# Grouped-query attention on one core: the last job's exponentials, the closing checks, the last store and the general path's loads moved between engines

## The chip, the core and the metric

The kernel runs on one core of a Trainium2 chip. A core has five engines with queues of their own: TensorE (PE in the profile; its weight loads are PEld), VectorE (DVE), ScalarE (ACT), GpSimd (POOL) and SyncE (SP), which only issues DMAs here. Each engine takes its instructions in program order and waits for others by semaphores. Matrix products go to PSUM, which VectorE and ScalarE read; all else lies in SBUF.

The metric is the device time of one execution in microseconds (us), the median of several. Lower is better.

## What is computed

Attention with 32 query heads that share 8 heads of keys and values, four query heads to one; batch 8, sequence 512, head size 64, all in float32:

```python
K_expanded = np.repeat(K, heads_per_group, axis=2)
V_expanded = np.repeat(V, heads_per_group, axis=2)
scores = np.einsum('bhqd,bhkd->bhqk', Q, K_expanded) * scale     # scale = 1/sqrt(64)
weights = np.exp(scores - np.max(scores, axis=-1, keepdims=True))
weights = weights / (np.sum(weights, axis=-1, keepdims=True) + 1e-10)
output = np.einsum('bhqk,bhkd->bhqd', weights, V_expanded)       # heads moved to axis 1
```

The inputs are normally distributed random numbers.

## The kernel before, in words

There are two paths. `fast_path` computes the output without subtracting the maximum: it takes the exponential of the scaled scores as they are, in fp16. While it does so it checks that every row sum lies between `SUM_LO` and `SUM_HI`, and that the largest absolute value in V is at most `V_HI`. The checks end in one number, the tile `flag` ([1, 1]). After the fast path `values_load` (L54) loads the flag into a register of every engine, and `tc.If` (L55) jumps over `general_path`, which would compute everything again with the maximum subtracted. With these inputs the jump is always taken.

**Jobs.** The fast path is a loop over 64 jobs. Job j is one head of keys and values in one batch (u = j // 2 counts pairs of such heads, `b` is the batch, eight jobs to a batch), with its four query heads taken as two pairs, i = 0 and 1. One job needs 16 score blocks of 128 keys x 512 queries per half (`m`): for each pair i and key chunk kc of four, two matmuls (L221, two heads at a time in the upper and lower 64 rows) write a tile of 128 x 1024 in PSUM.

**Exponentials.** Most tiles go to ScalarE, one ACTIVATE for each tile of 1024 columns (`act_tile`, L239), which writes `pt` in fp16. The PSUM pool `sps` has two such tiles. A few blocks of pair 1 go to VectorE and GpSimd instead (`taken(j)`: 2 blocks of 512 columns, or 3 in the even jobs from 8 on). These form the exponential from the bits of an fp16 number: VectorE makes `u` from the scores (`exp_d`, L250) and masks `f` (`exp_d2`, L271); GpSimd makes `g` and `w` (`correction`, L263 and L267); VectorE adds u and w and so writes those blocks of `pt` (`exp_d4`, L284), one job later. In job 63, the last, `by_pool` is false, and VectorE does g and w too, in the same job. With three blocks taken, ScalarE has seven tiles in a job, one of them half as wide; with two, seven full ones.

**Products with V.** `pv(j, i, lo, hi)` (L315) multiplies the blocks of `pt` with V, 32 small matmuls for each pair, 16 at a time in between the scores of the next job; a column of ones in V gives the row sums. `norm(j, i)` takes the reciprocal of the sums on VectorE (L358), multiplies (L362) into `osb`, and stores from SyncE's queue (`store`, L402): one store for each u, but in the last u one for each pair of heads. The order of keys in the products is written out in `blocks`.

**Checks.** `check_v` (L195) reduces a quarter of V's batch to its largest absolute value on VectorE. `check_sums` compares 16 norms' reciprocals at a time with both bounds (`in_bounds`, L326). After the norm that leaves `NLAST` = 3 more, the rest is checked, and `vmax` (L378), `okmin` (L380) and `okall` (L381) gather all that came before. `last_check`, called by the last norm between its reciprocal and its multiplication, compares the last three norms (24 columns) in two VectorE instructions, counts over the 128 partitions by a matmul with ones (L396), and the very last instruction reduces the counts to the flag by their minimum (L537).

**Order of work.** `tc.manual_schedule()` keeps each engine's instructions in the order in which the program emits them, so the loop body is the order, written out by hand. Within a job it is: scores for tile 0, blocks for VectorE, tile 1, a check of V, then the products of the job before between the tiles. Loads of Q, K and V are issued from GpSimd's queue, three jobs or more ahead; the transposed keys and the stores are on SyncE's.

**The close.** What follows the flag has the lines of the program's own frame: L54 is the load of the flag, L55 the jump and the semaphores that stand for the skipped branch, L650 the end of the program, at which all engines meet.

Of the kernel before, what the change touches and what calls it, by code (L numbers as in the profile page):

```python
# [3 lines left out]

# [7 lines left out]
FP32 = mybir.dt.float32  # L12
# [6 lines left out]
EXP = mybir.ActivationFunctionType.Exp  # L19
AX = mybir.AxisListType  # L20
# [13 lines left out]
V_HI = 1.0e15  # L34

# [4 lines left out]
@with_exitstack  # L40
def kernel(
    ctx: ExitStack,
    tc: tile.TileContext,
    Q: bass.AP,
    K: bass.AP,
    V: bass.AP,
    out: bass.AP,
):
    nc = tc.nc
    flag_pool = ctx.enter_context(tc.tile_pool(name="flag", bufs=1))  # L50
    flag = flag_pool.tile([1, 1], I32, name="flag")
    with ExitStack() as fast, tc.manual_schedule():
        fast_path(fast, tc, Q, K, V, out, flag)
    good = nc.values_load(flag, min_val=0, max_val=128)  # L54
    with tc.If(good < 128):  # L55
        general_path(tc, Q, K, V, out)


def fast_path(ctx, tc, Q, K, V, out, flag):
# [28 lines left out]
    ident = const_pool.tile([128, 128], BF16, name="ident")  # L88
# [45 lines left out]
    def d_tile():  # L134
        return d_pool.tile([128, 2, S], FP32, name="d_ps")
# [69 lines left out]
    def taken(j):  # L205
        return 3 if WIDE(j) else 2
# [8 lines left out]
    jobs, osb, invs, ends = {}, {}, {}, []  # L215
# [40 lines left out]
    def by_pool(j):  # L256
        return j < NJOB - 1

    def correction(engine, f, g, w):
        as_bits = engine is nc.gpsimd
        engine.tensor_scalar(  # L263
            out=g, in0=f, scalar1=-EXP_F1, scalar2=EXP_K * 2.0 ** (24 * as_bits),
            op0=ALU.add, op1=ALU.mult,
        )
        engine.tensor_tensor(out=w, in0=g, in1=f.bitcast(FP16) if as_bits else f, op=ALU.mult)  # L267

    def exp_d2(j):
        st = jobs[j]  # L270
        nc.vector.tensor_single_scalar(  # L271
            out=st["f"], in_=st["u"], scalar=1023, op=ALU.bitwise_and
        )
        if by_pool(j):
            exp_d3(j, nc.gpsimd)

    def exp_d3(j, engine):
        st = jobs[j]
        correction(engine, st["f"], st["g"], st["w"])
# [13 lines left out]
    def blocks(j, i):  # L293
        if j == NJOB - 1:
            kcs = (0, 1, 2, 3) if i == 0 else (2, 0, 1, 3)
# [27 lines left out]
    def in_bounds(outs, inv, first):  # L323
        ops = ((1.0 / SUM_HI, ALU.is_ge), (1.0 / SUM_LO, ALU.is_le))
        for out_, in1, (bound, op) in zip(outs, (first, outs[0]), ops):
            nc.vector.scalar_tensor_tensor(  # L326
                out=out_, in0=inv, scalar=bound, in1=in1, op0=op, op1=ALU.mult
            )
# [11 lines left out]
    NLAST = 3  # L340
    inv_last = const_pool.tile([128, NLAST, 2, SC], FP32, name="inv_last")

    def norm(j, i):
# [15 lines left out]
        if left == 1:  # L359
            last_check()  # L360
        h = g * HPG + 2 * i
        nc.vector.tensor_tensor(  # L362
            out=osb[u][:, :, h:h + 2, :].rearrange("p qc m d -> p m qc d"),
            in0=sums[:, :, :, 0:D],
            in1=inv[:, :, :, None].to_broadcast((128, 2, SC, D)),
            op=ALU.mult,
        )
# [18 lines left out]
    def last_check():  # L386
        cols = NLAST * 2 * SC
        part = const_pool.tile([128, cols], FP32, name="part")
        right = const_pool.tile([128, cols], BF16, name="right")
        in_bounds(  # L390
            (part, right),
            inv_last.rearrange("p s m qc -> p (s m qc)"),
            okall[:, :].to_broadcast((128, cols)),
        )
        count = pv_pool.tile([128, 2, S], FP32, name="pv")
        nc.tensor.matmul(count[0:1, 0, 0:cols], ones, right, start=True, stop=True)  # L396
        ends.append(count[0:1, 0, 0:cols])

    def store(u, lo, hi):
        b, gp = divmod(u, GP)  # L400
        h0 = gp * 2 * HPG
        nc.sync.dma_start(  # L402
            out=out[b, :, h0 + lo:h0 + hi, :].rearrange("(sc p) h d -> p sc h d", p=128),
            in_=osb[u][:, :, lo:hi, :],
        )

# [39 lines left out]
    for j in range(NJOB):  # L446
        end = j == NJOB - 1
# [42 lines left out]
        if not end:  # L490
            bank = d_tile() if j else pv_tile()
            beside = act_tile(j, 4, bank) if taken(j) > 2 else None

            ahead = (j + 1,) if j < 6 else (7, 8) if j == 6 else (j + 2,)
            for n, to in enumerate(ahead):
                if to < NJOB:
                    reads.append(trans_q(to, bank[:, n, :], other=beside))
            if j == 0:
                reads.append(first_keys(1, bank[:, 1, :]))
            elif j == 1:  # L500
                reads.append(first_k(1, 1, bank[:, 1, :]))
            elif j > 1 and b == 0 and gp + 1 < GP:
                reads.append(first_k(gp + 1, g, bank[:, 1, :]))
        else:
            pv(j, 0, 0, 16)
        copies = [] if by_pool(j) else [read() for read in reads]
        if late and by_pool(last):
            exp_d4(last)
        check_sums()
        exp_d2(j)  # L510
        if not by_pool(j):
            exp_d3(j, nc.vector)
            exp_d4(j)
        else:
            copies = [read() for read in reads]
# [5 lines left out]
        if not end and taken(j + 1) > 2:  # L521
            exp_d(j + 1, 2, taken(j + 1), bank[:, 1:2, :], copies[0])()
# [9 lines left out]
        if end:  # L532
            pv(j, 0, 16, 32)
            norm(j, 0)
            pv(j, 1, 0, 32)
            norm(j, 1)
    nc.vector.tensor_reduce(out=flag, in_=ends[0], op=ALU.min, axis=AX.X)  # L537


def general_path(tc, Q, K, V, out):  # L540
# [8 lines left out]
    with ExitStack() as ctx:  # L549
        one = ctx.enter_context(tc.tile_pool(name="g_one", bufs=1))  # L550
        sb = ctx.enter_context(tc.tile_pool(name="g_sb", bufs=2))
        ps = ctx.enter_context(tc.tile_pool(name="g_ps", bufs=2, space=PS))
        ident = one.tile([128, 128], BF16, name="g_ident")
        make_identity(nc, ident)
        with tc.For_i(0, B, 1) as b:
            with tc.For_i(0, KV, 1) as g:
                k_nat = sb.tile([128, SC, D], BF16, name="g_k")
                v_nat = sb.tile([128, SC, D], BF16, name="g_v")
                for tile_, src in ((k_nat, K), (v_nat, V)):
                    nc.gpsimd.dma_start(  # L560
                        out=tile_,
                        in_=src[bass.ds(b, 1), :, bass.ds(g, 1), :].rearrange(
                            "o (sc p) g d -> p (o sc) (g d)", p=128
                        ),
                    )
                kt_ps = ps.tile([64, SC, 128], BF16, name="g_t")
# [4 lines left out]
                with tc.For_i(0, HPG, 1) as i:  # L571
                    q_nat = sb.tile([128, SC, D], BF16, name="g_q")
                    nc.gpsimd.dma_start(
                        out=q_nat,
# [3 lines left out]
                    )  # L578
                    o_sb = sb.tile([128, SC, D], FP32, name="g_o")
# [75 lines left out]
```

## Time and profile before

| | before |
|---|---|
| median of 3 runs | 417.14 us (417.1 to 418.14) |
| the profiled execution | 417.43 us |
| its span in the profile | 415.8 us |
| granted TensorE clock over the span | 0.996 |
| ScalarE busy | 400.6 us (96%) |
| PE busy (modelled) | 378.1 us (91%) |
| VectorE busy | 342.6 us (82%) |
| GpSimd busy | 301.5 us (73%) |

How to read the rows below. In a group of the page stand the line, the engine, the operation, the tiles written and read with their shapes, and the count; then the busy time in us and the mean of one in ns; then the engine's idle time ahead of them and what ended most of it. In the timeline stand the start in us, the length in us (of several instructions merged, from the first start to the last end), then the group. An engine's name with a q, as POOLq, is its queue: loads of registers, jumps, semaphores and the issue of DMAs, which do not count as busy. Records of one engine overlap, since each holds the instruction's whole way through the engine.

### The profile page before, as it was taken

Reading aid. Unit: us, or ns where it says so; the run is one execution under the profiler, and the core shown is the slowest. Engines: PE = TensorE matmul, PEld = TensorE weight load, DVE = VectorE, ACT = ScalarE, POOL = GpSimd, SP = SyncE. Lnnn points to the kernel's source line nnn. Section 1 sums busy time; section 2 is a strip of 40 time slices with the busy share of each in tenths; the row PEclk is TensorE's granted clock in tenths of the full one; section 3 lists DMA queues with packets and bytes.
Section 4 is the critical chain, followed back from the end, with each engine's and each line's share of the span. In section 5 each row is a group of like instructions: output and inputs, shape, how many; then the busy total and the mean of one; then the engine's idle time right before and its main releaser. Section 6 shows DMA issues by size and latency. Waiting matters only on the chain.

```text
span 415.8 us, 13054 instructions
## 1 busy us (share of the span) xinstructions
PE 378.1 (91%) x5681; PEld 233.7 (56%) x5681; DVE 342.6 (82%) x609; ACT 400.6 (96%) x449; POOL 301.5 (73%) x213
## 2 busy tenths in 40 slices
PE   5899999999999999999999999999999999999983
PEld 2555655555655555655655655555655555655652
DVE  3677888888888888988888888888889888898875
ACT  3999999999999999999999999999999999999992
POOL 9677665887678886797776897587876887667550
PEclk9999999999999999999999999999999999999998
DMA  9999976799849997399974999669995899732223
GB/s 136 162 165 188 191 154 153 107 214 187 171 139 205 127 222 160 114 217 130 240 181 94 208 180 215 159 85 219 188 173 151 173 160 213 162 110 102 102 102 107
DMA packets 91966, 67.20 MB, mean 162 GB/s; under 512 B 52097, under 2 KB 75137, under 8 KB 91905
## 3 DMA queue, kind: packets, MB, share of 16 engines
q0 software_dynamic: 55488, 24.91, 51.8%
q1 hardware_dynamic: 35888, 41.16, 36.1%
q8 instruction: 45, 0.74, 0.7%
q10 hardware_dynamic: 528, 0.26, 0.2%
q14 instruction: 17, 0.13, 0.1%
HBM read 50.33 MB, written 33.55 MB: 202 GB/s over the span
## 4 chain that ended last, share of the span: by engine, by line
ACT 84%; PE 10%; DVE 3%; issue 1%; DMA 1%; ACTq 0%; DVEq 0%
ACT pt L239 84%; PE s_ps L221 6%; PE pv L315 3%; DMA kf<-in_K_dram 1%; DVE o_sb L362 1%; DVE pt L284 1%; PE pv L185 1%; PE d_ps L185 1%; DVE qt L189 0%; DVE ok L326 0%; ACTq L239 0%; DVE w L267 0%; DVE f L271 0%; PE d_ps L146 0%; DVE twice L153 0%
## 5 line engine op out<-in xcount | busy, mean ns | idle before, releaser
L239 ACT ACTIVATE pt<-s_ps 128x1024 f16<-128x1024 f32 x420 | 397.4, 1289 | 6.1 <-PE s_ps L221 6.1
L315 PEld LDWEIGHTS <-pt 128*128 128x128 f16 x4096 | 142.1, 98 | 75.7 <-issue 56.1
L315 PE MATMUL pv<-v,pt 128*128 128x65 bf16 x4032 | 178.2, 195 | 1.0 <-DVE o_sb L362 0.5
L267 POOL TENSOR_TENSOR w<-g,f 128x1024 bf16<-128x1024 bf16 (+1 forms) x63 | 161.0, 2555 | 5.2
L221 PE MATMUL s_ps<-qt,kt 64*128 64x512 bf16 x728 | 142.6, 383 | 22.3 <-ACT pt L239 16.3
L263 POOL TENSOR_SCALAR g<-f 128x1024 bf16<-128x1024 int16 (+1 forms) x63 | 77.4, 1229 | 96.6 <-DVE f L271 96.6
L250 DVE TENSOR_SCALAR u<-d_ps 128x1024 int16<-128x1024 f32 (+1 forms) x92 | 96.8, 1052 | 1.1 <-PE d_ps L221 1.1
L362 DVE TENSOR_TENSOR o_sb<-pv,inv 128x512 f32<-128x512 f32 x125 | 86.4, 691 | 4.3
L221 PEld LDWEIGHTS <-kt 64*128 64x128 bf16 x896 | 51.8, 93 | 62.3 <-issue 34.9
L358 DVE RECIPROCAL inv<-pv 128x8 f32<-128x8 f32 x125 | 25.9, 207 | 54.6 <-PE pv L315 54.5
L284 DVE TENSOR_TENSOR pt<-u,w 128x1536 uint16<-128x1536 int16 (+1 forms) x64 | 51.1, 798 | 0.1
L221 PE MATMUL d_ps<-qt,kt 64*128 64x512 bf16 x168 | 43.0, 375 | 0.0
L189 DVE COPY qt<-d_ps 128x1024 bf16<-128x1024 bf16 x62 | 42.3, 684 | 0.0
L185 PEld LDWEIGHTS <-q_nat 128*128 128x128 bf16 x512 | 29.3, 99 | 21.1 <-issue 20.0
L185 PE MATMUL d_ps<-ident,q_nat 128*128 128x128 bf16 x496 | 38.3, 220 | 0.0
L271 DVE TENSOR_SCALAR f<-u 128x1536 int16<-128x1536 int16 (+1 forms) x64 | 30.6, 478 | 0.0
L114 POOL DMA_DIRECT2D v<-in_V_dram x32 | 29.0, 909 | 0.1
L129 POOL DMA_DIRECT2D q_nat<-in_Q_dram x33 | 27.0, 818 | 0.2 <-issue 0.2
L221 PE MATMUL s_ps<-qt,kt_first 64*128 64x512 bf16 x112 | 23.1, 407 | 4.2 <-ACT pt L239 3.0
L239 ACT ACTIVATE pt<-d_ps 128x512 f16<-128x512 f32 x28 | 25.2, 899 | 0.0
L195 DVE TENSOR_REDUCE okv<-v 128x1 f32<-128x512 bf16 x32 | 21.6, 676 | 0.0
L221 PEld LDWEIGHTS <-kt_first 64*128 64x128 bf16 x128 | 7.9, 95 | 11.9 <-issue 8.3
(52 smaller groups left out, 44.5 us busy)
## 6 DMA issues: line engine op xcount, KB each, us to landing
out_dram<-o_sb SPq DMA_DIRECT2D x31, 1024.0 KB, 6.8
q_nat<-in_Q_dram POOLq DMA_DIRECT2D x31, 512.0 KB, 6.2
k_nat<-in_K_dram POOLq DMA_DIRECT2D x7, 512.0 KB, 8.3
v<-in_V_dram POOLq DMA_DIRECT2D x28, 128.0 KB, 7.5
kt<-kt SPq DMA_DIRECT2D x14, 256.0 KB, 4.6
out_dram<-o_sb SPq DMA_DIRECT2D x4, 256.0 KB, 2.4
kt<-k_nat SPq DMA_TRANSPOSE x28, 5.8
v<-in_V_dram POOLq DMA_DIRECT2D x4, 96.0 KB, 8.4
```

Of the source, the lines that this page charges most:

```text
L114: nc.gpsimd.dma_start(out=vt[b % 2][:, sc, lo:hi, 0:D], in_=V[b, sc * 128:(sc + 1) * 128, lo:hi, :],)
L185: nc.tensor.transpose(ps[:, i, sc, :], qn[u][:, sc, h:h + 2, :], ident), other
L189: return lambda: apart(nc.vector.tensor_copy(out=qt[u][:, g, lo:hi, :], in_=ps[:, lo:hi, :, :].rearrange("p i sc c -> p i (sc c)")), other)
L221: return nc.tensor.matmul(ps, keys[64 * m:64 * m + 64, g if u == 0 else g ^ m, kc * 128:(kc + 1) * 128], qt[u][64 * m:64 * m + 64, g, i, : ...
L239: return nc.scalar.activation(out=jobs[j]["pt"][:, i, kc, lo:, :], in_=ps[:, lo:, :], func=EXP, scale=scale)
L250: return lambda: nc.vector.tensor_scalar(out=st["u"][:, lo:hi, :], in0=ps[:, 0:hi - lo, :], scalar1=A_U, scalar2=B_U, op0=ALU.mult, op1=AL ...
L263: engine.tensor_scalar(out=g, in0=f, scalar1=-EXP_F1, scalar2=EXP_K * 2.0 ** (24 * as_bits), op0=ALU.add, op1=ALU.mult,)
L267: engine.tensor_tensor(out=w, in0=g, in1=f.bitcast(FP16) if as_bits else f, op=ALU.mult)
L271: nc.vector.tensor_single_scalar(out=st["f"], in_=st["u"], scalar=1023, op=ALU.bitwise_and)
L284: nc.vector.tensor_tensor(out=st["pt"][:, DPAIR, :, :, :].rearrange("p kc m q -> p (kc m) q")[:, 0:n, :].bitcast(U16), in0=st["u"], in1=st ...
L315: nc.tensor.matmul(st["pv"][i][:, m, qc, :], st["pt"][:, i, kc, m, qc * 128:(qc + 1) * 128], vt[b % 2][:, kc, 2 * gp + g, :], start=(n < 2 ...
L362: nc.vector.tensor_tensor(out=osb[u][:, :, h:h + 2, :].rearrange("p qc m d -> p m qc d"), in0=sums[:, :, :, 0:D], in1=inv[:, :, :, None].t ...
```

## The change

- **Job 63** is taken out of the loop and written out behind it. Nothing of it goes to VectorE (`taken(63)` is 0): ScalarE computes its eight full tiles. `by_pool`, `correction` and `exp_d3` go, since only job 63 used their other branch. The key order of its products is 0, 1, 2, 3 for both pairs.
- **Checks.** `NLAST` is 7, so the gathering (`vmax`, `okmin`, `okall`) follows the norm of pair 0 of job 60, in the loop's job 61, instead of the norm of pair 0 of job 62; `last_check` covers 56 columns. The four checks of V's last batch stand in jobs 56, 57, 58 and 59 instead of 56, 58, 60 and 62.
- **The last check** runs on GpSimd (two `tensor_scalar`), TensorE (two matmuls that add into one count) and ScalarE (a Copy that sums the counts into the flag). The flag becomes a float, and the jump compares its bits with those of the full count, 256 x 56; the run-time check of the loaded value's range is left out.
- **The last store** is made in two halves of the query rows: two multiplications, the first half's store from SyncE's queue, the second half's from ScalarE's.
- **The general path** loads from SyncE's queue, in float32 and with a copy to bf16 on VectorE, where GpSimd's queue loaded and converted. It uses the fast path's identity matrix, which moves to the pool of the flag.

The core of the diff:

```diff
-    flag = flag_pool.tile([1, 1], I32, name="flag")
+    flag = flag_pool.tile([1, 1], FP32, name="flag")
+    ident = flag_pool.tile([128, 128], BF16, name="ident")
...
-    good = nc.values_load(flag, min_val=0, max_val=128)
-    with tc.If(good < 128):
-        general_path(tc, Q, K, V, out)
+    bits = int.from_bytes(struct.pack("<f", 256.0 * LAST_SUMS), "little")
+    good = nc.values_load(
+        flag.bitcast(I32), min_val=0, max_val=bits,
+        skip_runtime_bounds_check_because="a sum of ones and zeros, only compared with its largest value",
+    )
+    with tc.If(good < bits):
+        general_path(tc, Q, K, V, out, ident)
...
     def taken(j):
-        return 3 if WIDE(j) else 2
+        return 0 if j == NJOB - 1 else 3 if WIDE(j) else 2
...
-    NLAST = 3
+NLAST = 7
+LAST_SUMS = NLAST * 2 * 4
...
-        nc.vector.tensor_tensor(
-            out=osb[u][:, :, h:h + 2, :].rearrange("p qc m d -> p m qc d"),
-            in0=sums[:, :, :, 0:D],
-            in1=inv[:, :, :, None].to_broadcast((128, 2, SC, D)),
-            op=ALU.mult,
-        )
-        if u == NU - 1:
-            store(u, h, h + 2)
-        elif g == 1 and i == NPAIR - 1:
+        for n_, (lo, hi) in enumerate(((0, 2), (2, 4)) if left == 1 else ((0, 4),)):
+            nc.vector.tensor_tensor(
+                out=osb[u][:, lo:hi, h:h + 2, :].rearrange("p qc m d -> p m qc d"),
+                in0=sums[:, :, lo:hi, 0:D],
+                in1=inv[:, :, lo:hi, None].to_broadcast((128, 2, hi - lo, D)),
+                op=ALU.mult,
+            )
+            if u == NU - 1:
+                store(u, h, h + 2, lo, hi, nc.scalar if n_ else nc.sync)
+        if u < NU - 1 and g == 1 and i == NPAIR - 1:
             store(u, 0, 2 * HPG)
...
     def last_check():
         cols = NLAST * 2 * SC
-        part = const_pool.tile([128, cols], FP32, name="part")
-        right = const_pool.tile([128, cols], BF16, name="right")
-        in_bounds(
-            (part, right),
-            inv_last.rearrange("p s m qc -> p (s m qc)"),
-            okall[:, :].to_broadcast((128, cols)),
-        )
+        seen = const_pool.tile([1, cols], FP32, name="seen")
         count = pv_pool.tile([128, 2, S], FP32, name="pv")
-        nc.tensor.matmul(count[0:1, 0, 0:cols], ones, right, start=True, stop=True)
-        ends.append(count[0:1, 0, 0:cols])
+        for n, (bound, op) in enumerate(((1.0 / SUM_HI, ALU.is_ge), (1.0 / SUM_LO, ALU.is_le))):
+            right = const_pool.tile([128, cols], BF16, name=f"right{n}")
+            nc.gpsimd.tensor_scalar(
+                out=right, in0=inv_last.rearrange("p s m qc -> p (s m qc)"),
+                scalar1=bound, scalar2=okall, op0=op, op1=ALU.mult,
+            )
+            nc.tensor.matmul(
+                count[0:1, 0, 0:cols], ones, right, start=(n == 0), stop=(n == 1)
+            )
+        nc.scalar.activation(
+            out=seen, in_=count[0:1, 0, 0:cols], func=COPY, accum_out=flag
+        )
...
-        if g == (b < B - 1) and j > 1:
+        if g == 1 and 1 < j and b < B - 1:
             check_v(b, gp)
+        if 0 <= j - 8 * (B - 1) < SC:
+            check_v(B - 1, j - 8 * (B - 1))
...
+    j, last = NJOB - 1, NJOB - 2
+    open_job(j)
+    act_tile(j, 0)
+    act_tile(j, 1)
+    pv(last, 0, 0, 16)
+    act_tile(j, 2)
+    pv(last, 0, 16, 32)
+    norm(last, 0)
+    act_tile(j, 3)
+    exp_d4(last)
+    check_sums()
+    pv(j, 0, 0, 16)
+    act_tile(j, 4)
+    pv(last, 1, 0, 16)
+    act_tile(j, 5)
+    pv(last, 1, 16, 32)
+    norm(last, 1)
+    act_tile(j, 6)
+    pv(j, 0, 16, 32)
+    norm(j, 0)
+    act_tile(j, 7)
+    pv(j, 1, 0, 32)
+    norm(j, 1)
...
                 for tile_, src in ((k_nat, K), (v_nat, V)):
-                    nc.gpsimd.dma_start(
-                        out=tile_,
+                    as_is = sb.tile([128, SC, D], FP32, name="g_in")
+                    nc.sync.dma_start(
+                        out=as_is,
...
+                    nc.vector.tensor_copy(out=tile_, in_=as_is)
```

More of the change, by code (lines that the diff above doesn't have):

```diff
@@ L3 @@
 import math
+import struct
 import concourse.bass as bass
@@ L489, in fast_path @@
         reads = []
[L490 to L507, printed above, removed]
+        bank = d_tile() if j else pv_tile()
+        beside = act_tile(j, 4, bank) if taken(j) > 2 else None
+        ahead = (j + 1,) if j < 6 else (7, 8) if j == 6 else (j + 2,)
+        for n, to in enumerate(ahead):
+            if to < NJOB:
+                reads.append(trans_q(to, bank[:, n, :], other=beside))
+        if j == 0:
+            reads.append(first_keys(1, bank[:, 1, :]))
+        elif j == 1:
+            reads.append(first_k(1, 1, bank[:, 1, :]))
+        elif j > 1 and b == 0 and gp + 1 < GP:
+            reads.append(first_k(gp + 1, g, bank[:, 1, :]))
+        if late:
             exp_d4(last)
@@ L510, in fast_path @@
         exp_d2(j)
[L511 to L515, printed above, removed]
+        copies = [read() for read in reads]
         if taken(j) == 2:
```

63 lines of the change are left out of this document (25 added, 38 removed).

## The prediction, before the changed kernel was run

> **What bounds the kernel now.** I read the page first, then the timeline of the last three jobs engine by engine, then the rows of the closing lines (L54, L55, L650).
>
> ```profile
> span 415.8 us, 13054 instructions
> ...
> PE 378.1 (91%) x5681; PEld 233.7 (56%) x5681; DVE 342.6 (82%) x609; ACT 400.6 (96%) x449; POOL 301.5 (73%) x213
> ...
> L239 ACT ACTIVATE pt<-s_ps 128x1024 f16<-128x1024 f32 x420 | 397.4, 1289 | 6.1 <-PE s_ps L221 6.1
> ...
> out_dram<-o_sb SPq DMA_DIRECT2D x4, 256.0 KB, 2.4
> ```
>
> ScalarE works 96% of the span and is idle for only 6.1 us before its exponentials: the steady part is its stream. The change gives that stream no other work before job 63, so what it can move is the end. There, the timeline of ScalarE (start, us, instructions merged) and of VectorE:
>
> ```profile
> 386.92 12.35 ACT L239 ACTIVATE pt<-s_ps 128x1024 f16<-128x1024 f32 x13
> ...
> 399.33 8.76 ACT L239 ACTIVATE pt<-s_ps 128x1024 f16<-128x1024 f32 x9
> ```
>
> ```profile
> 404.43 0.56 DVE L326 SCALAR_TENSOR_TENSOR ok<-inv,ok 128x104 f32<-128x104 f32 x2
> ...
> 405.43 0.96 DVE L284 TENSOR_TENSOR pt<-u,w 128x1536 uint16<-128x1536 int16 x1
> 406.30 0.42 DVE L271 TENSOR_SCALAR f<-u 128x1024 int16<-128x1024 int16 x1
> 406.75 0.43 DVE L263 TENSOR_SCALAR g<-f 128x1024 bf16<-128x1024 int16 x1
> 407.22 0.69 DVE L267 TENSOR_TENSOR w<-g,f 128x1024 bf16<-128x1024 bf16 x1
> 408.01 0.69 DVE L284 TENSOR_TENSOR pt<-u,w 128x1024 uint16<-128x1024 int16 x1
> ...
> 410.30 0.20 DVE L358 RECIPROCAL inv_last<-s_ps 128x8 f32<-128x8 f32 x1
> 410.54 0.18 DVE L326 SCALAR_TENSOR_TENSOR part<-inv_last,okall 128x24 f32<-128x24 f32 x1
> 410.75 0.18 DVE L326 SCALAR_TENSOR_TENSOR right<-inv_last,part 128x24 bf16<-128x24 f32 x1
> 410.86 0.68 DVE L362 TENSOR_TENSOR o_sb<-s_ps,inv_last 128x512 f32<-128x512 f32 x1
> 411.45 0.16 DVE L537 TENSOR_REDUCE flag<-pv 1x1 int32<-1x24 f32 x1
> ```
>
> ScalarE is done at 408.09. VectorE sets the pace of the end: bounds checks at 404.43, job 62's pt at 405.43, then job 63's own chain f, g, w, pt up to 408.70, the normalisations, the last check, and the flag at 411.61. The span ends 4.2 us after the flag, and in them no engine computes:
>
> ```profile
> L54 POOLq TENSOR_LOAD <-flag x1: 730/730/730, 411.7 to 411.7; - x1
> ```
>
> ```profile
> L55 POOLq EVENT_SEMAPHORE  x2: 17/30/43, 412.9 to 413.0; - x2
> L55 POOLq COMPARE_BRANCH  x1: 45/45/45, 412.4 to 412.4; - x1
> L55 POOLq INC_SWDGE_SEM  x1: 496/496/496, 413.1 to 413.1; - x1
> ```
>
> ```profile
> L650 SPq EVENT_SEMAPHORE  x12: 28/28/28, 413.6 to 414.2; - x12
> L650 SPq DRAIN  x2: 7/10/13, 414.3 to 414.4; - x2
> L650 POOLq DRAIN  x1: 1302/1302/1302, 413.6 to 413.6; - x1
> L650 POOLq EVENT_SEMAPHORE  x1: 17/17/17, 415.0 to 415.0; - x1
> ```
>
> The columns are the shortest, median and longest in ns, then first and last start in us. GpSimd loads the flag, jumps over the general path, runs INC_SWDGE_SEM (0.50) and a DRAIN of 1.30, and its semaphore at 415.0 opens the common close, 0.8 us long. SyncE is ready at 414.4, 0.6 earlier. So the end hangs on two things: **when the flag is there, and what GpSimd does after it.**
>
> **The change part by part.**
>
> *Job 63 all on ScalarE.* VectorE loses u, and f, g, w, pt from 406.30 to 408.70. ScalarE gets an eighth full tile. A tile's step is (12.35 - 1.29)/12 = 0.92, from the row of thirteen and the mean of one. By it, nine tiles from 399.33 end at 399.33 + 1.29 + 8 x 0.92 = 407.98, ten at 408.90; the real 408.09 holds a stall of 0.1, in which job 63's scores sit on PE behind products that wait for job 62's pt. That pt comes 1.0 earlier (next part), so the stall goes. PE needs the eighth tile for eight products alone:
>
> ```profile
> 407.86 0.41 PE L315 MATMUL s_ps<-v,pt 128*128 128x65 bf16 x8
> 408.76 0.91 PE L315 MATMUL s_ps<-v,pt 128*128 128x65 bf16 x24 [0.49 <-DVE pt L284]
> 411.08 0.17 PE L396 MATMUL pv<-right,ones 128*1 128x24 bf16 x1 [1.41 <-DVE right L326]
> ```
>
> With 0.05 to see the tile (0.06 from pt's end at 408.70 to 408.76), 0.41 for the eight and as little to the reciprocal, the last reciprocal starts at 409.40 for 410.30: **-0.9 us**. What is late next is ScalarE itself; the 24 products before those eight wait for tile 6, at 407.98, whose PSUM buffer they take, and with 0.91 they end as the last tile does.
>
> *Checks moved.* The chain from 404.43 to 405.43 (1.0 us) goes behind job 60's first normalisation, in job 61, a little shorter there (72 columns for 104): 0.93. Queued behind it on VectorE is job 60's pt, and behind that, on PE:
>
> ```profile
> 393.42 0.41 PE L315 MATMUL pv<-v,pt 128*128 128x65 bf16 x8
> 393.82 0.39 PE L221 MATMUL s_ps<-qt,kt 64*128 64x512 bf16 x2
> ```
>
> ```profile
> 392.02 0.95 DVE L284 TENSOR_TENSOR pt<-u,w 128x1536 uint16<-128x1536 int16 x1
> ```
>
> The pt starts at 392.95 and ends at 393.90. Three of the eight products read it, so the scores start near 394.15 for 393.82 and are there at 394.55. By the step, the tile before theirs ends at 386.92 + 1.29 + 7 x 0.92 = 394.65, so ScalarE still finds them in time. I cost it at nothing; the cover is 0.1 us, and without it at most the whole 0.93 falls on ScalarE. V's four checks go from jobs 56, 58, 60 and 62 to jobs 56 to 59. The odd jobs of the earlier batches carry one each, and ScalarE's 6.1 us of idleness in all leaves no room for a stall by them: nothing.
>
> *The last check.* Now 410.30 to 411.61, 1.31 us: reciprocal, two checks, PE, and a reduction queued behind the 0.68 multiplication. After: reciprocal, two GpSimd checks of 56 columns, two PE counts, a ScalarE copy that sums. The trace has neither that check nor that copy; nearest:
>
> ```profile
> L263 POOL TENSOR_SCALAR g<-f 128x1536 bf16<-128x1536 int16 x28 | 41.0, 1466 | 47.9 <-DVE f L271 47.9
> ...
> L263 POOL TENSOR_SCALAR g<-f 128x1024 bf16<-128x1024 int16 x35 | 36.4, 1039 | 48.6 <-DVE f L271 48.6
> ```
>
> These two give 0.83 ns a column and 0.185 us fixed, so 56 columns take 0.23. Ends: 0.18 (VectorE's check) and 1.04 (the 1024 columns); I take 0.23, the line through the nearest rows, and 0.09 to start. The Trainium skill (GPSIMD Engine Reference, Key points) speaks against this move: for elementwise work VectorE is about twice as fast. The row of 1039 against VectorE's 0.43 for the same g agrees. By the rule, an estimate, two checks would take 0.72 instead of 0.46, and the gain below be 0.26 less. For the summing copy the ends are 0.16 (the reduction of 24 columns) and 0.92 (a tile's step); I take 0.37, nearer the first. In all 0.20 + 0.09 + 2 x 0.23 + 0.15 (right to count) + 0.17 (count) + 0.04 + 0.37 = 1.48: the flag stands at 410.88 for 411.61, **-0.7 us**.
>
> *Store in halves.* Two multiplications take the place of 0.68, ending about 410.1 and 410.4. SyncE issues one half then, ScalarE the other behind its copy, by 411.0. A last store needs 2.4 us to land, so 413.4, beside SyncE's waits up to T + 2.4 (rival 1): nothing, or 0.1 if late. Behind ScalarE's copy wait only this half and its flag load.
>
> *General path.* Its loads go from GpSimd's queue to SyncE's, with copies on VectorE; none runs here. Left is the bookkeeping of the skipped branch: INC_SWDGE_SEM and the semaphore before it should go, from 413.0 to 413.6 on GpSimd, **-0.6 us**. Ends: 0, if it stays; -1.0, where SyncE is last instead. The range check of the flag goes from SyncE, hidden behind GpSimd. The identity moves pools: nothing.
>
> **Sum.** Flag at 410.88, then 4.17 - 0.6 = 3.57: span 414.45, or -1.3 us. The profiled run took 417.43, 1.6 outside its span and 0.3 over the median; taken from the median, 417.14 - 1.3 = 415.8 us.
>
> **Rivals.**
> 1. *GpSimd leaves the end*: it no longer loads the flag, or its DRAIN shrinks with INC_SWDGE_SEM. SyncE is last: load 0.73, jump 0.5, twelve semaphores 0.7, 0.5 between them, so T + 2.4 with T the flag, and the close of 0.8: 414.1, -1.7, **415.4 us**. For it: the branch holds no GpSimd instruction any more. Against: the flag is loaded for all engines, and the 1.30 may belong to the kernel's own GpSimd DMAs.
> 2. *GpSimd's close stays as it is*, so the general path's edit does not do what it seems to: -0.7 alone, **416.4 us**.
> 3. *The moved work bites*: job 61 stalls ScalarE, or GpSimd's checks or the copy lie at their far ends; 0.4 to 1.0 of the 1.3 is lost, **416.5 us**.
> 4. *Slower*: SyncE's skipped code grows by three loads in loops, and its jump lands on code that is not there yet. Price: a fetch like the last store's landing, 2.4 us. SyncE is ready at T + 4.8, the end at 416.5, +0.7, **417.8 us**. It decides from 0.3 us on, SyncE's slack to GpSimd, and turns the sign at 1.7. Against: today's jump takes 0.5 us (412.4 to 412.9). The Trainium skill (Runtime: NRT & Kernel Launch, Instruction fetch mechanics) says that a taken branch out of the prefetched window waits for such a fetch; no jump of this trace shows one.
>
> **How the numbers follow.** Forecast 0.40, rival 1 0.25, rival 2 0.14, rival 3 0.13, rival 4 0.08. A measurement of this kernel tells about 0.3% from no change, 1.25 us, so below 415.89 is faster. The forecast, uncertain by 0.4 from the flag's chain, is there six times in ten, 0.24; rival 1 nearly whole, 0.24; a little of rival 2: faster 0.50. Slower by over 0.3% needs rivals 3 and 4 together: 0.05. The range runs from rival 1 with quicker checks, 414.9, to rival 3 with its loss of 1.0 and 0.2 of spread, 417.0; it leaves out rival 4 and the tails.
>
> **What would show it.** Right: ScalarE's last tile ends near 408.9, with no gap in job 63; the last reciprocal starts near 409.4, the flag is there at 410.9; no INC_SWDGE_SEM at the branch; GpSimd's DRAIN still 1.3 and last. Wrong: a gap ahead of ScalarE's tiles between 394 and 398; GpSimd checks over 0.4 each; SyncE's semaphores after GpSimd's DRAIN; a jump of 2 us.

## The result, and the profile after

The median is 416.51 us after for 417.38 before, taken side by side on one chip: a ratio of 0.9982 with a 95% interval of 0.9974 to 0.9991. The kernel is 0.8 us faster by the ratio (0.4 to 1.1 by its interval), some six tenths of the 1.3 that was forecast. The profiled execution took 416.19 us and its span is 414.2. The page of the changed kernel has these rows for those shown of before:

```profile
span 414.2 us, 13052 instructions
...
PE 377.8 (91%) x5682; PEld 233.5 (56%) x5682; DVE 339.1 (82%) x602; ACT 401.8 (97%) x452; POOL 302.5 (73%) x215
...
L247 ACT ACTIVATE pt<-s_ps 128x1024 f16<-128x1024 f32 x421 | 398.0, 1281 | 5.7 <-PE s_ps L229 5.6
...
out_dram<-o_sb SPq DMA_DIRECT2D x3, 256.0 KB, 2.2
```

ScalarE has one tile more (421 for 420), VectorE 3.5 us of work less. As before, the end decides. The timeline of ScalarE there:

```profile
398.68 0.59 ACT L247 ACTIVATE pt<-d_ps 128x512 f16<-128x512 f32 x1
399.15 9.28 ACT L247 ACTIVATE pt<-s_ps 128x1024 f16<-128x1024 f32 x10
410.60 0.21 ACT L396 ACTIVATE seen<-pv 1x56 f32<-1x56 f32 x1 [2.17 <-PE pv L393]
410.67 0.40 ACTq L403 DMA_DIRECT2D out_dram<-o_sb  x1
410.72 0.18 ACT L396 ACTIVATION_READ_ACCUMULATOR seen<-pv 1x1 f32 x1
```

Ten tiles run in one piece to the end of job 63; the row names no idle time. Then ScalarE waits 2.17 us for the counts, and the flag is there when the accumulator has been read, at 410.90. VectorE, GpSimd and PE between the last tile and the flag:

```profile
408.95 0.21 DVE L354 RECIPROCAL inv_last<-s_ps 128x8 f32<-128x8 f32 x1 [1.19 <-PE s_ps L312]
409.19 0.76 DVE L359 TENSOR_TENSOR o_sb<-s_ps,inv_last 128x256 f32<-128x256 f32 x2
```

```profile
409.27 1.06 POOL L389 TENSOR_SCALAR right<-inv_last,okall 128x56 bf16<-128x56 f32 x2 [5.10 <-DVE inv_last L354]
```

```profile
409.80 0.19 PE L393 MATMUL pv<-right,ones 128*1 128x56 bf16 x1 [0.89 <-POOL right L389]
410.38 0.19 PE L393 MATMUL pv<-right,ones 128*1 128x56 bf16 x1 [0.39 <-POOL right L389]
```

The two GpSimd checks fill 1.06 us, and PE counts each as it comes, 0.58 us apart. Behind the flag stand its load (L60), the jump (L64) and the close (L664):

```profile
L60 POOLq TENSOR_LOAD <-flag x1: 493/493/493, 410.9 to 410.9; - x1
```

```profile
L64 SPq EVENT_SEMAPHORE  x4: 17/17/17, 412.0 to 412.3; - x4
L64 SPq COMPARE_BRANCH  x1: 58/58/58, 411.5 to 411.5; - x1
L64 POOLq COMPARE_BRANCH  x1: 45/45/45, 411.5 to 411.5; - x1
```

```profile
L664 SPq DRAIN  x2: 7/10/13, 413.1 to 413.1; - x2
L664 POOLq EVENT_SEMAPHORE  x2: 17/17/17, 413.4 to 413.5; - x2
L664 POOLq DRAIN  x1: 1380/1380/1380, 412.0 to 412.0; - x1
```

GpSimd has no INC_SWDGE_SEM at the branch any more; its DRAIN starts at 412.0 and is still the last thing to end, 0.2 after SyncE's second.

**Where the time went.** One profile of a kernel and another differ by chance ahead of the last jobs: ScalarE's 401st exponential ended at 366.20 before and at 365.67 after, and between 365.63 and 366.95 in the experiments. Of what the change moves, only one check of V (364.88) stands ahead of it, and no exponential is shifted by that check. So the pair is read in pieces that begin at that exponential. R is the start of the last reciprocal, T the moment when the flag is written, E the end of the span; the last column is the time of an execution less its span, as a mean over all measured executions (e4, e8 and e9 have one each). Experiments e1 to e9 are below.

| kernel | 401st tile to R | R to T | T to E | outside the span |
|---|---|---|---|---|
| before | 44.10 | 1.31 | 4.17 | 1.67 |
| after | 43.28 | 1.95 | 3.28 | 2.00 |
| e1, last check on VectorE | 43.27 | 1.28 | 3.48 | 1.86 |
| e2, GpSimd's loads | 43.28 | 1.95 | 3.82 | 1.70 |
| e3, one whole store | 43.28 | 1.95 | 3.32 | 2.01 |
| e4, check without operand | 43.28 | 1.77 | 3.27 | 2.08 |
| e5, loads alone | 44.09 | 1.31 | 3.74 | 1.79 |
| e6, job 63 alone | 43.71 | 1.32 | 3.93 | 1.81 |
| e7, e1 with one store | 43.27 | 1.29 | 3.79 | 2.21 |
| e8, probes | 43.27 | 1.94 | 3.27 | 2.05 |
| e9, addition for comparison | 43.43 | 1.48 | 3.26 | 1.94 |

A fifth piece lies at the very start. Three views show it: GpSimd's register moves in the frame's line L639 of the kernel before, then the first row of PE's timeline before, then the same row after.

```profile
L639 POOLq MOVE  x2: 29/34/39, 0.2 to 0.3; - x2
```

```profile
1.33 1.03 PE L438 MATMUL s_ps<-warm 128*128 128x512 bf16 x2 [1.33 <-DVE warm L435]
```

```profile
1.21 1.03 PE L440 MATMUL s_ps<-warm 128*128 128x512 bf16 x2 [1.21 <-DVE warm L437]
```

After the change the moves stand on SyncE, GpSimd is at the common start 0.12 earlier, and so is everything behind it. Added up: -0.12 at the start, -0.82 to the reciprocal, +0.64 to the flag, -0.89 to the end, +0.33 outside, in all -0.86. The medians differ by 0.87 and the ratio says 0.75 (0.4 to 1.1); that the first agrees so closely is chance, since the pieces come from one profile of each kernel.

### The profile page after: what moved, and what is told of

Read it like the earlier page. It is cut to its first block, busy times and chain, and to the rows that moved or that the text cites. A ratio compares the mean times of both kernels' runs of the same rounds, so it can differ in the third digit from the quotient of the medians.

```text
span 414.2 us, 13052 instructions
## 1 busy us (share of the span) xinstructions
PE 377.8 (91%) x5682; PEld 233.5 (56%) x5682; DVE 339.1 (82%) x602; ACT 401.8 (97%) x452; POOL 302.5 (73%) x215
## 4 chain that ended last, share of the span: by engine, by line
ACT 83%; PE 11%; DVE 3%; issue 1%; DMA 1%; ACTq 0%; POOL 0%
ACT pt L247 83%; PE s_ps L229 6%; PE pv L312 3%; DMA kf<-in_K_dram 1%; DVE o_sb L359 1%; PE pv L193 1%; PE d_ps L193 1%; DVE pt L281 0%; DVE qt L197 0%; PE s_ps L312 0%; DVE u L258 0%; POOL right L389 0%; ACTq L247 0%; DVE ok L323 0%; PE d_ps L154 0%
## 5 line engine op out<-in xcount | busy, mean ns | idle before, releaser
L258 DVE TENSOR_SCALAR u<-d_ps 128x1024 int16<-128x1024 f32 (+1 forms) x91 | 95.6, 1050 | 1.1 <-PE d_ps L229 1.1
L359 DVE TENSOR_TENSOR o_sb<-pv,inv 128x512 f32<-128x512 f32 x121 | 83.7, 691 | 4.2
L281 DVE TENSOR_TENSOR pt<-u,w 128x1024 uint16<-128x1024 int16 (+1 forms) x63 | 50.4, 800 | 0.2 <-POOL w L274 0.2
L267 DVE TENSOR_SCALAR f<-u 128x1024 int16<-128x1024 int16 (+1 forms) x63 | 30.2, 479 | 0.0
```

The costliest lines, as they stand in the source:

```text
L258: return lambda: nc.vector.tensor_scalar(out=st["u"][:, lo:hi, :], in0=ps[:, 0:hi - lo, :], scalar1=A_U, scalar2=B_U, op0=ALU.mult, op1=AL ...
L267: nc.vector.tensor_single_scalar(out=st["f"], in_=st["u"], scalar=1023, op=ALU.bitwise_and)
L281: nc.vector.tensor_tensor(out=st["pt"][:, DPAIR, :, :, :].rearrange("p kc m q -> p (kc m) q")[:, 0:n, :].bitcast(U16), in0=st["u"], in1=st ...
L359: nc.vector.tensor_tensor(out=osb[u][:, lo:hi, h:h + 2, :].rearrange("p qc m d -> p m qc d"), in0=sums[:, :, lo:hi, 0:D], in1=inv[:, :, lo ...
```

## The experiments

The first question was what the last check costs on GpSimd; e1, e4, e8 and e9 ask it. The others undo or isolate one part.

**e1: the last check on VectorE.** The changed kernel, with the two comparisons of before in place of GpSimd's, and so one count and a full count of 128 x 56 for the jump:

```diff
-        for n, (bound, op) in enumerate(((1.0 / SUM_HI, ALU.is_ge), (1.0 / SUM_LO, ALU.is_le))):
-            right = const_pool.tile([128, cols], BF16, name=f"right{n}")
-            nc.gpsimd.tensor_scalar(
-                out=right, in0=inv_last.rearrange("p s m qc -> p (s m qc)"),
-                scalar1=bound, scalar2=okall, op0=op, op1=ALU.mult,
-            )
-            nc.tensor.matmul(
-                count[0:1, 0, 0:cols], ones, right, start=(n == 0), stop=(n == 1)
-            )
+        in_bounds(
+            (part, right),
+            inv_last.rearrange("p s m qc -> p (s m qc)"),
+            okall[:, :].to_broadcast((128, cols)),
+        )
+        nc.tensor.matmul(count[0:1, 0, 0:cols], ones, right, start=True, stop=True)
```

> The changed kernel with the last check's two comparisons back on VectorE (56 columns, one count on TensorE, ScalarE still sums it into the flag). In the changed kernel the flag stands 1.95 us after the last reciprocal starts, where 1.48 was forecast. Theory: GpSimd's two comparisons, 0.48 each and 0.58 apart, are the whole of the difference; then VectorE's pair (0.22 a step) gives reciprocal to flag 1.35, and the span is 0.6 shorter. Rival: the count and the summing copy set the flag, or the multiplications, now 0.45 later, hold the end by their stores; then reciprocal to flag stays above 1.7, or the span shrinks by less than 0.3.

Measured: 415.95 us, ratio to the kernel before 0.9966 (0.9954 to 0.9977). R to T is 1.28. VectorE's two checks, and the close of this kernel:

```profile
L323 DVE SCALAR_TENSOR_TENSOR part<-inv_last,okall x1: 217/217/217, 410.3 to 410.3; 128x56 f32<-128x56 f32 x1
L323 DVE SCALAR_TENSOR_TENSOR right<-inv_last,part x1: 216/216/216, 410.6 to 410.6; 128x56 bf16<-128x56 f32 x1
```

```profile
L663 SPq DRAIN  x2: 7/10/13, 414.0 to 414.0; - x2
L663 POOLq EVENT_SEMAPHORE  x2: 17/17/17, 414.1 to 414.1; - x2
L663 POOLq DRAIN  x1: 1375/1375/1375, 412.4 to 412.4; - x1
```

Each check takes 0.22 where GpSimd's takes 0.48, so the flag comes 0.67 earlier after the reciprocal. Of that 0.20 is lost behind it: GpSimd's DRAIN ends at 413.8, but SyncE drains at 414.0 and is last. ScalarE's half of the store, issued at 411.48, lands at 413.45, and SyncE, which goes from one semaphore to the next in 0.06 otherwise, has its next only at 413.47. So the theory held for the flag, but the end came 0.47 earlier and not 0.6, by what the rival said of the stores. With 0.14 less outside the span this version is about 0.6 us faster than the change. It is the fastest of those that were measured more than once; its interval and that of the change just touch.

**e2: the general path's loads back on GpSimd's queue**, all else as changed (Q's load likewise):

```diff
-                    as_is = sb.tile([128, SC, D], FP32, name="g_in")
-                    nc.sync.dma_start(
-                        out=as_is,
+                    nc.gpsimd.dma_start(
+                        out=tile_,
...
-                    nc.vector.tensor_copy(out=tile_, in_=as_is)
```

> The changed kernel with the general path's loads back on GpSimd's queue (none of it runs). From the flag to the end of the span the kernel before takes 4.17 us and the changed one 3.28. Theory: INC_SWDGE_SEM and the semaphores ahead of it, 0.7 together, come back and nothing else, so flag to end is 3.95 to 4.0 with the flag's loads still 0.49. Rival: the shorter flag load (0.73 before, 0.49 after) belongs to this edit too; then 4.15 to 4.2. Second rival: nothing comes back, 3.3, and the gain is from the missing range check.

Measured: 417.02 us, ratio 0.9993 (0.998 to 1.0005). Line L64 has its instruction back:

```profile
L64 POOLq EVENT_SEMAPHORE  x1: 43/43/43, 413.3 to 413.3; - x1
...
L64 POOLq INC_SWDGE_SEM  x1: 496/496/496, 413.3 to 413.3; - x1
```

T to E grows by 0.54, to 3.82, less than the theory's 3.95: the DRAIN goes from 1.38 back to 1.30, and only one of the two semaphores that line L55 of before shows on GpSimd returns. The flag's load stays at 0.50, so the rival is out. The start grows by its 0.12. But outside the span 0.30 comes back: 1.70, as before, for 2.00. By these pieces the edit is worth 0.66 inside the span and 0.36 in all; the two ratios differ by 0.46 us, and their intervals overlap.

**e3: the last store whole**, all else as changed:

```diff
-        for n_, (lo, hi) in enumerate(((0, 2), (2, 4)) if left == 1 else ((0, 4),)):
+        for n_, (lo, hi) in enumerate(((0, 4),)):
```

> The changed kernel with its last multiplication and store whole again, the store on SyncE's queue. Theory: the two halves are worth nothing by themselves, since no engine waits for their landing; the span stays within 0.1. Rival: the engines' loads of the flag took 0.73 before because the last store was being issued and read out beside them; then they go from 0.49 back to about 0.7 and the end is 0.2 later. Second rival: the whole store, issued 0.35 later than the first half, lands after SyncE's last waits and holds the end by 0.1 to 0.3.

Measured: 416.54 us, ratio 0.9986 (0.9975 to 0.9997). T to E is 3.32 for 3.28. With the flag so late, the halves buy nothing: SyncE is done 0.2 ahead of the end of GpSimd's DRAIN either way.

**e4: GpSimd's check multiplied by the constant 1.0 instead of `okall`**, so that V's check and the earlier sums are left out of the flag:

```diff
-                scalar1=bound, scalar2=okall, op0=op, op1=ALU.mult,
+                scalar1=bound, scalar2=1.0, op0=op, op1=ALU.mult,
```

> The changed kernel with GpSimd's two comparisons multiplied by the constant 1.0 instead of the column okall, so that the flag leaves out V's check and the earlier sums. Theory: an operand read per partition makes the comparison cost 0.48 instead of the 0.23 read from the line through g's rows; then each takes 0.23 to 0.25 and reciprocal to flag goes from 1.95 to 1.45. Rival: a short GpSimd instruction on float32 costs near 0.5 whatever its operands; then nothing changes.

Measured: 416.95 us in a single execution, R to T 1.77. GpSimd's group:

```profile
L389 POOL TENSOR_SCALAR right<-inv_last 128x56 bf16<-128x56 f32 x2 | 0.8, 410 | 5.2 <-DVE inv_last L354 5.1
```

The operand that differs from partition to partition costs 0.07 for each check, 0.18 in the chain. So neither the theory (1.45) nor its rival (no change) held: at 0.41 the checks are still far over the 0.23 of the forecast's line. Three causes were open then: a fixed cost of any short GpSimd instruction, the float32 input, or the comparison.

**e8: six probes on GpSimd in job 63**, their results unused:

```diff
+    for n, (src, cols, ops) in enumerate((
+        (warm.bitcast(I16), 56, (ALU.add, ALU.mult)),
+        (ok, 56, (ALU.add, ALU.mult)),
+        (ok, 56, (ALU.is_ge, ALU.mult)),
+        (warm.bitcast(I16), 512, (ALU.add, ALU.mult)),
+        (ok, 128, (ALU.add, ALU.mult)),
+        (ok, 128, (ALU.is_ge, ALU.mult)),
+    )):
+        probe = const_pool.tile([128, cols], BF16, name=f"probe{n}")
+        nc.gpsimd.tensor_scalar(
+            out=probe, in0=src[:, 0:cols], scalar1=0.5, scalar2=2.0, op0=ops[0], op1=ops[1]
+        )
```

> The changed kernel with six more short GpSimd instructions in job 63, their results unused, to price the 0.41 to 0.48 us of the two checks of 56 columns: add and multiply on 56 columns of int16; the same on 56 columns of float32; the comparison and multiply on 56 of float32; add and multiply on 512 columns of int16; then 128 columns of float32, add and comparison. The line of the forecast (0.83 ns a column and 0.185 fixed, int16) gives 0.23 for the first and 0.61 for the 512. Theory A (a fixed cost of about 0.4 for any short GpSimd instruction): all three of 56 columns take 0.40 to 0.45. Theory B (float32 input is what costs): the int16 takes 0.23 to 0.3, both float32 0.4. Theory C (the comparison costs): only the third takes 0.4. The two of 128 columns give the cost of a column.

Measured, in two views of the probes' line (in the second: the shortest, median and longest of a group in ns):

```profile
404.67 1.00 POOL L547 TENSOR_SCALAR probe<-warm 128x56 bf16<-128x56 int16 x1
405.64 0.61 POOL L547 TENSOR_SCALAR probe<-ok 128x56 bf16<-128x56 f32 x2
406.22 0.61 POOL L547 TENSOR_SCALAR probe<-warm 128x512 bf16<-128x512 int16 x1
406.80 0.89 POOL L547 TENSOR_SCALAR probe<-ok 128x128 bf16<-128x128 f32 x2
```

```profile
L547 POOL TENSOR_SCALAR probe<-ok x4: 232/351/631, 405.6 to 407.1; 128x56 bf16<-128x56 f32 x2, 128x128 bf16<-128x128 f32 x2
```

The 512 columns of int16 take 0.61, which is the forecast's line to the hundredth. Of the four probes on float32 the shortest is the addition on 56 columns, 0.232, again on the line; the longest is the comparison on 128, 0.631. So neither a fixed cost nor the float32 input explains 0.41: theory C stands. The first probe, the 56 columns of int16, took 1.00 where 0.23 was due; it lies beside an addition of VectorE (see the last section).

**e9: an addition in place of the last comparisons**, so that the bounds of the last seven norms are left out of the flag, and probes with a line each:

```diff
-                scalar1=bound, scalar2=okall, op0=op, op1=ALU.mult,
+                scalar1=bound + 2.0, scalar2=okall, op0=ALU.add, op1=ALU.mult,
```

> The changed kernel with the comparison of GpSimd's two last checks replaced by an addition of the same shape, types and operand, so that the last seven norms' bounds are left out of the flag; and with six unused probes in job 63, after a spacer of 512 columns: 56 columns of int16 add, float32 add, float32 add with the per-partition operand, float32 comparison, float32 comparison with the operand. Theory (the comparison itself costs about 0.2, the operand 0.07): probes 0.23, 0.23, 0.30, 0.41, 0.48; the two real ones take 0.30 each, follow each other at 0.38 instead of 0.58, and the flag is there 1.57 after the last reciprocal starts, for 1.95. Rival (whatever stands at the end of a chain, with a wait ahead and a semaphore behind, takes 0.4 to 0.5): the probes add at 0.23, but the two real ones stay at 0.4 or more and the flag at 1.8 or more.

Measured: GpSimd's groups in these microseconds.

```profile
L389 POOL TENSOR_SCALAR right<-inv_last,okall 128x56 bf16<-128x56 f32 x2 | 0.6, 312 | 2.4 <-DVE inv_last L354 2.4
L561 POOL TENSOR_SCALAR probe<-ok,okall 128x56 bf16<-128x56 f32 x1 | 0.5, 465 | 0.0
L558 POOL TENSOR_SCALAR probe<-ok 128x56 bf16<-128x56 f32 x1 | 0.4, 415 | 0.0
L555 POOL TENSOR_SCALAR probe<-ok,okall 128x56 bf16<-128x56 f32 x1 | 0.3, 306 | 0.0
L552 POOL TENSOR_SCALAR probe<-ok 128x56 bf16<-128x56 f32 x1 | 0.2, 231 | 0.0
```

From the bottom: addition 0.23, addition with the operand 0.31, comparison 0.42, comparison with the operand 0.47. The comparison costs 0.18 and the operand 0.05 to 0.08, and the two real instructions, with additions in them, fall to 0.31; the rival is out. They start 0.29 apart and not 0.38 as expected, so R to T is 1.48 for the theory's 1.57. That settles what made the checks dear: mainly the comparison, and the operand with it. (The 43.43 to the reciprocal comes from the probes: job 62's `pt` is longer beside them, as the last section shows, and the last exponential ends 0.15 later.)

**e5: the general path's loads on SyncE's queue, alone**: the kernel before with this one part. It is the reverse of e2's diff, and the general path uses the fast path's identity matrix besides, as in the change; in e2 that stays.

> The kernel before with one part of the change: the general path's loads on SyncE's queue, with the copies to bf16 on VectorE. Theory (this edit saves inside the span and gives half of it back outside): INC_SWDGE_SEM is gone, the span from flag to end is 4.17 - 0.54 = 3.6 us, the time outside the span rises from 1.67 to about 2.0, so the time falls by 0.2 to 0.3 us only, to about 416.9 for 417.15. Rival (the time outside the span belongs to something else): outside stays at 1.67 and the time falls with the span, by 0.55, to 416.6. The reciprocal to flag stays at 1.31.

Measured: 416.75 us, ratio 0.9992 (0.9983 to 1.0001). Line L651 is the close here:

```profile
L651 SPq DRAIN  x2: 7/10/13, 414.0 to 414.1; - x2
L651 POOLq DRAIN  x1: 1376/1376/1376, 412.5 to 412.5; - x1
L651 POOLq EVENT_SEMAPHORE  x1: 17/17/17, 414.1 to 414.1; - x1
```

GpSimd's DRAIN now ends at 413.9, but SyncE drains up to 414.1: it still stores a whole tile at the flag, loads the flag 0.3 later than the others and runs its range check. So alone the edit takes 0.43 off T to E, not 0.54. The first product stands at 1.21, as after the change. Outside the span 0.11 is added. The pieces give 0.12 + 0.43 - 0.11 = 0.44 of gain and the ratio 0.33, between the theory's 0.2 to 0.3 and the rival's 0.55, and the time's interval holds both. So neither stands as it was put: less is saved inside the span than either said, and less given back outside it than the theory said.

**e6: job 63 on ScalarE, alone**: the kernel before with the written-out last job, `taken(63)` = 0 and the plain key order, and nothing else of the change:

```diff
-        return 3 if WIDE(j) else 2
+        return 0 if j == NJOB - 1 else 3 if WIDE(j) else 2
...
+NLAST = 3
```

> The kernel before with job 63 written out and all on ScalarE, and nothing else: three norms left to the last check on VectorE, V's checks and the gathering where they were, one whole last store, GpSimd's loads in the general path. Theory of the prediction (the moved checks earn something by making job 62's pt early): the 1.0 us of checks still stands ahead of job 62's pt, the products that need it hold up job 63's scores, ScalarE has a gap in job 63 and the last reciprocal gains 0.4 instead of 0.82 (43.7 us from ScalarE's tile 400, for 44.10 before and 43.28 after). Rival (the moved checks are worth nothing by themselves): no gap, 43.3. In both, 1.31 from the reciprocal to the flag and 4.2 from there to the end, 1.67 outside the span; time 416.7 by the theory, 416.3 by the rival.

Measured: 416.92 us, ratio 0.9991 (0.9982 to 1.0), 43.71 to the reciprocal. ScalarE, VectorE and PE in job 63:

```profile
399.33 7.76 ACT L243 ACTIVATE pt<-s_ps 128x1024 f16<-128x1024 f32 x8
407.46 1.95 ACT L243 ACTIVATE pt<-s_ps 128x1024 f16<-128x1024 f32 x2 [0.36 <-PE s_ps L225]
```

```profile
404.43 0.56 DVE L319 SCALAR_TENSOR_TENSOR ok<-inv,ok 128x104 f32<-128x104 f32 x2
...
405.42 0.96 DVE L277 TENSOR_TENSOR pt<-u,w 128x1536 uint16<-128x1536 int16 x1
```

```profile
406.44 0.66 PE L308 MATMUL pv<-v,pt 128*128 128x65 bf16 x16 [0.73 <-DVE pt L277]
407.03 0.39 PE L225 MATMUL s_ps<-qt,kt 64*128 64x512 bf16 x2
```

The chain of waits can be read off: the checks hold VectorE from 404.43, so job 62's pt is done at 406.38; PE waits 0.73 for it, the scores behind it come late, and ScalarE has a gap of 0.36. The last job alone gains 0.39, as the theory said. The other 0.43 of the change's 0.82 is put down to the moved checks: e1, e2 and e3 show that the other parts leave this piece at 43.27 to 43.28. Not as expected are the 3.93 from flag to end, for 4.2, and the 1.81 outside the span, for 1.67.

**e7: e1 with one whole last store** (e3's diff on e1):

> The kernel with the last check on VectorE (e1) and one whole last store on SyncE's queue instead of two halves. Theory (with the flag earlier, SyncE's waits for the last landings are near the end of the span, and a whole store lands no earlier than the later half): the store is issued at about the flag, lands 2.3 us behind it, SyncE ends 2.6 behind the flag, and the time is within 0.1 us of e1's: 3.5 us from flag to end. Rival (halves matter once the flag is early): the whole store lands 0.3 or more later and the end with it, 3.8 us.

Measured: 416.36 us, ratio 0.9984 (0.9973 to 0.9994), T to E 3.79 for e1's 3.48. The close:

```profile
L663 SPq DRAIN  x2: 7/10/13, 414.2 to 414.3; - x2
L663 POOLq DRAIN  x1: 1375/1375/1375, 412.4 to 412.4; - x1
```

The theory falls, the rival holds: the whole store lands 2.8 us after the flag instead of 2.1, SyncE waits for it, and the end is 0.3 later. Inside the span the halves are worth nothing beside the GpSimd check and 0.3 without it. The time outside the span is 0.35 longer here than in e1; why is open.

## Why the prediction was partly right

The direction, the likeliest mechanism and the range held: 416.51 was measured for 415.8 in a range of 414.9 to 417.0. The interval of the ratio lies below 1, but its difference of 0.18% is within the 0.3% that the prediction took as its bound: by that, the outcome is the "no difference" that it gave 0.45, and not the "faster" that it gave 0.50. The forecast gain of 1.3 was too large by about 0.5. One step, the flag's chain, was off by 0.47 alone; that the sum is off by no more is luck, since the other misses (+0.08, -0.12, -0.29 and +0.33, below) cancel.

- **Job 63 on ScalarE, -0.9**: measured -0.82. The last tile was to end at 408.90 with no gap; it ends at 408.44, and 408.97 with the 0.53 by which this profile is early, without a gap. The prediction saw that job 62's pt had to come earlier, but sized the stall by the 0.1 of the kernel before. With an eighth tile in the job it would have been 0.36 (e6): half the gain hung on the moved checks (e6 and its difference to the change).
- **Checks moved, nothing**: right. Job 60's pt, made in job 61, was forecast from 392.95 to 393.90 and the scores at 394.15. The changed kernel has this, half a microsecond early as a whole:

```profile
391.49 0.49 DVE L323 SCALAR_TENSOR_TENSOR ok<-inv,ok 128x72 f32<-128x72 f32 x2
...
392.42 0.96 DVE L281 TENSOR_TENSOR pt<-u,w 128x1536 uint16<-128x1536 int16 x1
```

```profile
393.43 0.26 PE L312 MATMUL pv<-v,pt 128*128 128x65 bf16 x3 [0.21 <-DVE pt L281]
393.63 0.39 PE L229 MATMUL s_ps<-qt,kt 64*128 64x512 bf16 x2
```

  PE does wait 0.21 for pt, three products stand behind it as said, and the cover of 0.1 held: the tiles after it end at most 0.04 later, counted from the 401st.
- **The last check, flag 1.48 after the reciprocal's start**: this is the step that failed, by its size. It took 1.95. The price of a GpSimd check, 0.23, was taken from the line through two rows of another operation, an addition with constants. The line was right for additions (0.607 for 512 columns of int16 in e8, 0.231 for 56 of float32 in e9; no 56 columns of int16 ran undisturbed), but the check compares and takes an operand per partition: 0.48, and 0.58 from one to the next. So the two checks filled 1.06 where 0.46 was forecast. The rest of the chain took 0.89 where 1.02 was forecast: the count came 0.05 behind `right` and not 0.15, and the summing copy took 0.30 and not 0.37. This hid 0.13 of the miss. In e9 the two additions filled 0.60 and the rest 0.88, so that its 1.48 is the forecast's number by chance. In all, the check's move, taken with the copy, lost 0.64 where 0.17 was forecast, and the flag's gain of 0.7 shrank to 0.2 (0.82 less 0.64). The Trainium skill (GPSIMD Engine Reference, Key points) has VectorE about twice as fast for elementwise work, and e1 agrees for the check: 0.22 for 0.48 on the same 56 columns. For an addition of that size GpSimd took 0.23 to 0.31, and no run has VectorE's. The estimate of 0.72 that the prediction made by it was nearer to the measured 0.96 than the 0.46 it took.
- **Store in halves, nothing**: right beside the late flag (e3: 0.04), and only there (e7: 0.3 inside the span).
- **General path, -0.6**: INC_SWDGE_SEM and its semaphore went, as said; e2 gives 0.54 for it. "The identity moves pools: nothing" was likely wrong by 0.1: the other semaphore on GpSimd at line L55 of before stands 0.11 ahead of that one, in e6 too, where the general path still makes its own identity matrix on GpSimd, and in e2, where it doesn't, that semaphore is missing. The identity was not run alone. Two more things were not in the sum: GpSimd's register moves left the start, -0.12; and outside the span the time rose, by 0.11 when the edit is made alone and by 0.30 in the changed kernel. Why is open; no view of the profile shows that time, and the part of it that other edits make was not separated. That the flag's range check is hidden behind GpSimd was true of the kernel before only: in e5, with GpSimd earlier, SyncE is last.
- **Behind the flag, -0.89 for -0.6**: on GpSimd the time from its jump to its DRAIN went from 1.20 to 0.47, the DRAIN from 1.30 to 1.38, and the flag's load from 0.73 to 0.49. The load was not in the sum. It is 0.72 in e5 and 0.49 in e6, so it comes with job 63's move; why is open.

Of the rivals, the third names what happened in one of its parts: checks on GpSimd above 0.4, the sign that the prediction had set for being wrong. It was priced at 416.5 in all, and 416.51 was measured. That agreement is partly chance: the price starts from 417.14 for the kernel before, which stood at 417.38 beside the changed one, and the other misses cancel. The first did not come: the DRAIN stayed, at 1.38. In e1 a part of it did, SyncE's being last. The second is excluded by the missing INC_SWDGE_SEM. Of the fourth the rows show nothing: SyncE's jump at 411.5 is followed by its next instruction at 412.0, as GpSimd's of before took from 412.4 to 412.9.

## What to carry to other kernels

A price from a line through other rows holds for their operation, not only for their shape and engine: on GpSimd, where a comparison of 56 columns took 1.5 to 1.8 times as long as an addition, look for a row of the same operation, or let the range have the difference. When work leaves the engine that is last, write down who is next and by how little: here SyncE was done only 0.2 us ahead of GpSimd, and the halves of the store, worth nothing beside a late flag, are worth 0.3 inside the span when it is early. An edit to code that never runs can still move the time, by the moves and semaphores that it puts on an engine's queue at the start and at the jump (here 0.12 and 0.54 us, of which 0.30 came back outside the span).

## What the runs showed that was not expected

- GpSimd's comparison costs by the column. On float32, 56 columns took 0.415 and 128 took 0.631 (e8's longest): 3.0 ns a column, where the addition's line has 0.83.
- A short GpSimd instruction that begins beside a long 16-bit addition on VectorE ended, both times, only when that addition did, to within 0.1 us. The first probe of e8, 56 columns from 404.67, took 1.00 while VectorE's `pt` ran from 404.62 to 405.58. In e9 a spacer of 512 columns stood first, the same probe took 0.934 from 404.68, and `pt` itself was longer than its usual 0.96:

```profile
404.16 1.35 DVE L281 TENSOR_TENSOR pt<-u,w 128x1536 uint16<-128x1536 int16 x1 [0.18 <-POOL w L274]
```

  Neither engine's rows name a wait. Nothing was run to tell what the two share.
- The time outside the span is not a constant: 1.67 before, 2.00 after, 2.21 in e7. A verdict on a change of a microsecond at a kernel's end has to be taken from the whole time.
